# A retention head's output: copied to SBUF before it is normalised, backward scaled K on another engine, transposes back later

## The chip, the cores and the metric

The kernel runs on one core of a Trainium2 chip. A core has five engines with queues of their own: TensorE (PE, matmuls and transposes into PSUM), VectorE (DVE), ScalarE (ACT), GpSimd (POOL) and SyncE (SP, which issues the DMAs). [...] The metric is the time on the device of one execution in microseconds, the median of the runs shown.

## The reference

The kernel is one inference step of a backbone of two layers with 1024 features, on 128 prompt tokens and 512 sample tokens. Each layer normalises its input, projects it (`z = h @ w_in`), feeds three groups of mixers side by side (four retention heads, a Hyena convolution, a gated linear recurrence called RG-LRU), multiplies each by its SiLU gate and projects back. The change touches the retention heads. Each is computed in chunks of 128 tokens, forward and backward, and its output is normalised over the 128 features of the head:

```
scores = einsum('bnihd,bnjhd->bnhij', qc, kc) * dmat
inner  = einsum('bnhij,bnjhe->bnihe', scores, vc)
kv     = einsum('bnjhd,hj,bnjhe->bnhde', kc, zeta, vc)   # K scaled by zeta, per direction
cross  = einsum('bnihd,hi,bnhde->bnihe', qc, xi, R_prev) # R: running sum of kv
out    = of + ob[:, ::-1]
out    = out * lax.rsqrt(jnp.mean(out * out, axis=-1, keepdims=True) + EPS)
...
y = concat([ret_out * silu(g_r), hy_out * silu(g_h), lru_out * silu(g_l)])
```

## The kernel before

Both token groups are held together as 640 columns (five chunks of 128; with pads 644), features on the partitions. The input projection runs as a long row of matmuls: for each group of 128 output features (tile `z`) the two parts of the input (`hh`, `hl`) meet the two parts of the weights (`w_3h`, `w_3l` and so on). ScalarE rounds the weights for the high part, and GpSimd subtracts it for the low part (`split`, L830: a 128x1024 instruction for each group).

The order of TensorE's work is written out by hand: helpers `mm` (L332) and `tr` (L335) chain each matmul behind the one emitted before it and move a clock of estimated TensorE time; each mixer is a generator that yields how many microseconds of that clock to let pass before it emits its next step, and the `z` matmuls are emitted in between. Instructions of the other engines are put in order by the scheduler, by their place in the program and by a priority (`tc.high_priority`). ScalarE's work goes through one helper (`act`, L299), so that all of its rows have one line.

A retention head goes through these steps (`ret`, for layer `l` and head `h`; the tiles bear both numbers, so `rk01s` is layer 0, head 1):

- the input of a head, `ret_in`: Q and K are rotated by `rope` (VectorE L1161 and L1163, GpSimd L1162 between them);
- `rk`: K is transposed chunk by chunk into PSUM (512 columns in the tile that ends in `s`, 128 in the one that ends in `p`), and VectorE scales it into KF (forward) and KB (backward), L1199 and L1200;
- `rv`: V is transposed, and ScalarE copies it out;
- `rs`: the scores, multiplied by the decay mask on VectorE (L1218); `kv`: the chunk states, accumulated on VectorE (L1232); `ro`: the output, 3 matmuls a chunk, in PSUM;
- the normalisation: squares from PSUM on ScalarE, sums on VectorE (L1251, L1252), the power -1/2 on GpSimd (L1253), and the product of PSUM and that factor on VectorE, for 512 columns in L1254 and 128 in L1256;
- `rt`: the normalised output is transposed back and copied out by ScalarE; when both it and its gate are there, VectorE multiplies them (L1368), and the output projection reads the product at the end of the layer.

The tiles rk, rv, rs, kv, ro, rt and the gates of the RG-LRU (`lg`) take turns in four PSUM buffers; a new one waits until the readers of the oldest are done. The RG-LRU (`lru`) runs between the heads: gate matmuls `lg` (three for each group of ScalarE activations), products and two scans on VectorE (L1326 to L1349; L1342 and L1344 are the scans, L1349 adds them) and small copies of pads on GpSimd (L1337). L1208 is the scaling of Q on GpSimd. ScalarE loads a table when its function changes.

Of the kernel before, what the change touches and what calls it, by code (L numbers as in the profile page):

```python
# [12 lines left out]
AF = mybir.ActivationFunctionType  # L13
ALU = mybir.AluOpType
AX = mybir.AxisListType

P = 128
# [194 lines left out]
XQ, PW3, PA0, NA, NV, NQ, PO, PFO = 1, 0, 2, 14, 225, 1, 0, 1  # L212
PT0, PT1, PT2 = 2, 5, 8

PRI = 400
LTE, XSEQ, LA3, LH1_, LH2_, LA02, LHD, LHD0, LT0 = 2.5, 'FNAAAAAABANBAFBBBBABBB', 0.0, 3.5, 12.0, 16.0, 6.75, 76.25, 3.37
LT1, LF0, LF1, LC0, LC1, LA, LA0, LH0 = 6.25, 6.75, 3.25, 1.42, 1.31, 3.0, 11.75, 5.88
LH1, LV0, LV01, LV1, LV2, LV3, LV4, LVE, LP = 7.28, 7.5, 5.5, 3.12, 2.5, 1.71, 4.15, 9.0, 6.0
LRI, LR0, LR1, LR2, LR3, LLS, LLF, LL0 = 1.05, 1.71, 3.2, 5.7, 11.5, 1.25, 8.38, 2.83
# [5 lines left out]
def step_kernel(ctx: ExitStack, tc: tile.TileContext, xT, ada_w, w_in, w_out, vecs, fw1, fw2, fw3, lgw, sret,  # L225
                c_fwd, c_inv, c_ident, c_rope, c_ret, c_zfeat, c_win, o_y, o_ret, o_lru, dbg=None):
    nc = tc.nc
    V, S, G, T = nc.vector, nc.scalar, nc.gpsimd, nc.tensor
# [39 lines left out]
    def ar(off, n, p0=0, p1=P):  # L268
        if off >= RT_:
            return RT[0][p0:p1, off - RT_:off - RT_ + n]  # L270
        return A[p0:p1, off:off + n]
# [26 lines left out]
    def act(out, in_, f=AF.Identity, bias=0.0, scale=1.0):  # L298
        return S.activation(out, in_, f, bias=bias, scale=scale)  # L299
# [793 lines left out]
    zgs_ = [small(16) for _ in range(DEPTH)]  # L1093
# [57 lines left out]
    NO_ = SC_R + 640  # L1151
    SQ_ = ZB_ + 652
# [18 lines left out]
    read, out_, norm_ = {}, {}, {}  # L1171
# [23 lines left out]
    def ret(l, h):  # L1195
        pk, pkp = to_time(ar(K_, ZC), f"rk{l}{h}")
        for dst, i in ((KF_, h), (KB_, 4 + h)):
            with tc.high_priority(offset=PRI):
                V.tensor_scalar(ar(dst, 512), pk, ar(zgs_[l] + 2 * i, 1), None, op0=ALU.mult)  # L1199
                V.tensor_scalar(ar(dst + 512, 128), pkp, ar(zgs_[l] + 2 * i, 1), None, op0=ALU.mult)  # L1200
        if h == 0:
            yield LR1
        pv, pvp = to_time(ar(VC_, ZC), f"rv{l}{h}")
# [8 lines left out]
        for s0, blocks in ((0, (0, 1, 2, 3)), (4, (4,))):  # L1212
            nb = len(blocks)
            ps = pat(f"rs{l}{h}{s0}")
            for n in blocks:
                c = S0 + 128 * n if n < 4 else 0
# [28 lines left out]
        if h < 3:  # L1245
            ret_state(l, h + 1)
        out_[l, h] = True
        act(ar(SQ_, 512), ps, AF.Square)
        act(ar(SQ_ + 512, 128), pp[:, 0:128], AF.Square)
        v = ar(vr_, 5)  # L1250
        V.tensor_reduce(v, ar(SQ_, 640).rearrange("p (n c) -> p n c", n=5), axis=AX.X, op=ALU.add)  # L1251
        V.tensor_scalar(v, v, 1.0 / 128, EPS, op0=ALU.mult, op1=ALU.add)  # L1252
        G.tensor_tensor(v, v, ar(mh_, 5), op=ALU.pow)  # L1253
        i = V.tensor_tensor(ar(NO_, 512).rearrange("p (n c) -> p n c", n=4), ps.rearrange("p (n c) -> p n c", n=4),  # L1254
                        v[:, 0:4].unsqueeze(2).broadcast_to([P, 4, 128]), op=ALU.mult)
        norm_[l, h] = i, V.tensor_scalar(ar(NO_ + 512, 128), pp[:, 0:128], v[:, 4:5], None, op0=ALU.mult)  # L1256
        yield LR3
        pt, pp = pat(f"rt{l}{h}s"), pat(f"rt{l}{h}p")
        for n in range(5):
            tr(pt[:, 128 * n:128 * n + 128] if n < 4 else pp[:, 0:128], ar(NO_ + 128 * n, 128), ident)  # L1260
# [441 lines left out]
```

## Time and profile before

| what | value |
|---|---|
| median of 3 runs (lowest, highest) | 1303.76 us (1303.5, 1305.56) |
| the profiled execution: its own time, its span | 1307.67 us, 1305.9 us |
| mean granted TensorE clock | 0.955 of full speed |
| busy: PE, DVE, ACT, POOL | 1160.9, 893.0, 633.3, 595.5 us |
| stage of layer 0 that holds the retention heads | about 415 to 625 us of the span |
| the same stage of layer 1 | about 1025 to 1235 us |

The busy times are sums over the whole span; they don't say where an engine waits. The rows below are read by stage: the waits of one engine, the rows of an engine in order of time (its start, its duration, and in square brackets how long the engine stood idle before it and what ended the wait), and busy time with the granted clock by stretches. A row with x4 is four instructions.

### The profile page before, as it was taken

To read this page: it belongs to the slowest core of one execution; us is meant where nothing else is said; L and a number is where in the kernel's file an instruction comes from. 1 tells how busy PE (TensorE), PEld (TensorE's weight loads), DVE (VectorE), ACT (ScalarE), POOL (GpSimd) and SP (SyncE) were. 2 spreads that over 40 slices of the span, in tenths; PEclk is the share of its full clock that TensorE was granted. 3 is DMA by queue.
4 is the path that set the end of the run, shared out by engine and by line. 5 is a ranking of instruction groups with operands and counts; after the bars stand their busy time and mean duration, and the time that the engine had idled before them with its cause. 6 is when DMAs were issued, how large, how long until landed. Compare 5 with 4: busy or idle time off the path is not lost. (4 is left out here: it accounts for less than half of the span.)

```text
span 1305.9 us, 20607 instructions
## 1 busy us (share of the span) xinstructions
PE 1160.9 (89%) x7944; PEld 1099.8 (84%) x7944; DVE 893.0 (68%) x1382; ACT 633.3 (48%) x1120; POOL 595.5 (46%) x523
## 2 busy tenths in 40 slices
PE   4599988798999888898999899999999889889996
PEld 2478878797999888897787788999998889888996
DVE  5998983866776776777888775466467577666313
ACT  3566646564333765565566554332333367655220
POOL 1743335645556434524343355545355554344431
PEclk9799988999999888899999989999999899899998
DMA  9562213222121211243545464222221111213222
GB/s 336 205 204 74 77 65 143 92 91 98 55 73 48 65 35 47 79 141 115 166 145 185 130 213 136 73 80 89 66 88 42 61 49 57 65 43 120 72 62 81
DMA packets 53522, 132.80 MB, mean 102 GB/s; under 512 B 6358, under 2 KB 15590, under 8 KB 52144
## 3 DMA queue, kind: packets, MB, share of 16 engines
q1 hardware_dynamic: 53076, 131.38, 30.7%
q8 instruction: 62, 1.02, 0.3%
q14 instruction: 36, 0.29, 0.1%
q10 hardware_dynamic: 348, 0.11, 0.0%
HBM read 112.77 MB, written 18.70 MB: 101 GB/s over the span
## 5 line engine op out<-in xcount | busy, mean ns | idle before, releaser
L299 ACT ACTIVATE arena<-arena 128x644 f32<-128x644 f32 (+6 forms) x168 | 116.6, 722 | 80.1 <-DVE arena L1400 28.3
L299 ACT ACTIVATE r<-arena 128x512 fp32r<-128x512 f32 (+1 forms) x72 | 43.6, 605 | 90.1 <-DVE arena L519 34.2
L299 ACT ACTIVATE rt<-arena 128x512 fp32r<-128x512 f32 (+2 forms) x44 | 29.7, 674 | 76.0 <-POOL arena L983 50.5
L332 PE MATMUL u<-r,cfwd 128*128 128x256 f32 x432 | 61.6, 291 | 2.1 <-DVE r L544 1.9
L544 POOL TENSOR_TENSOR r<-arena,r 128x512 fp32r<-128x512 f32 (+1 forms) x24 | 29.3, 1220 | 70.0 <-ACT r L299 53.5
L332 PEld LDWEIGHTS u<-r,cfwd 128*128 128x128 f32 x432 | 57.4, 199 | 3.1 <-DVE r L544 2.5
L1400 DVE SCALAR_TENSOR_TENSOR arena<-o,arena 128x128 f32<-128x128 f32 (+3 forms) x34 | 16.7, 524 | 56.0 <-PE o L332 56.0
L332 PE MATMUL lg<-r 128*128 128x322 f32 x192 | 39.0, 360 | 10.4 <-DVE rt L1199 8.4
L978 DVE TENSOR_TENSOR arena<-u,arena 128x512 f32<-128x512 f32 x40 | 27.4, 686 | 30.1 <-PE u L332 30.1
L983 POOL TENSOR_TENSOR arena<-arena 128x256 f32<-128x256 f32 x40 | 37.0, 926 | 20.1 <-DVE arena L979 13.5
L332 PEld LDWEIGHTS lg<-r 128*128 128x128 f32 x192 | 35.5, 230 | 12.3 <-issue 8.9
L332 PE MATMUL spr<-r,cfwd 128*128 128x256 f32 x192 | 35.0, 293 | 11.1 <-ACT rt L299 6.4
L332 PE MATMUL spi<-r,cfwd 128*128 128x256 f32 x168 | 36.2, 304 | 7.0 <-ACT r L299 4.2
L986 POOL TENSOR_TENSOR rt<-arena,rt 128x512 fp32r<-128x512 f32 x24 | 31.2, 1302 | 24.0 <-ACT rt L299 24.0
L332 PEld LDWEIGHTS spr<-r,cfwd 128*128 128x128 f32 x192 | 27.8, 189 | 16.9 <-ACT rt L299 8.4
L299 ACT ACT_TABLE_LOAD x30 | 38.5, 1283 | 3.9 <-DMA arena<-in_vecs 3.4
L299 ACT ACTIVATE r<-rt 128x512 fp32r<-128x512 f32 (+3 forms) x50 | 28.2, 565 | 22.7 <-PE spi L332 11.7
L544 POOL TENSOR_TENSOR r<-rt,r 128x256 fp32r<-128x256 f32 (+1 forms) x16 | 19.7, 1229 | 42.6 <-ACT r L299 36.0
L544 POOL TENSOR_TENSOR dm<-rt,r 128x256 fp32r<-128x256 f32 (+1 forms) x16 | 22.5, 1408 | 33.7 <-ACT r L299 33.7
L299 ACT ACTIVATE arena<-lg,arena 128x322 f32<-128x322 f32 x64 | 30.9, 529 | 14.4 <-PE lg L332 13.9
L1319 POOL MEMSET arena<- 128x2 f32 x32 | 2.1, 100 | 77.9 <-ACT arena L299 77.9
L332 PEld LDWEIGHTS spi<-r,cfwd 128*128 128x128 f32 x168 | 27.9, 200 | 11.4 <-ACT r L299 4.9
(1266 smaller groups left out, 4177.6 us busy)
## 6 DMA issues: line engine op xcount, KB each, us to landing
w<-in_w_in SPq DMA_DIRECT2D x80, 512.0 KB
aw<-in_ada_w SPq DMA_DIRECT2D x96, 256.0 KB
wo<-in_w_out SPq DMA_DIRECT2D x32, 384.0 KB
spec<-arena SPq DMA_DIRECT2D x16, 640.0 KB
arena<-spec SPq DMA_DIRECT2D x8, 1280.0 KB
arena<-in_xT SPq DMA_DIRECT2D x16, 320.0 KB
rt<-in_c_win SPq DMA_DIRECT2D x4, 640.0 KB
arena<-xspill SPq DMA_DIRECT2D x8, 320.0 KB
```

The source lines that it names most:

```text
L299: return S.activation(out, in_, f, bias=bias, scale=scale)
L332: return queue(T.matmul(out, lhs, x, start=start, stop=stop), w * n / 2400 * (4 if x.dtype == F32 else 1))
L544: eng.tensor_tensor(lo, src, f(h), op=ALU.subtract)
L978: V.tensor_tensor(y, pv, hre[:, c].unsqueeze(1).broadcast_to([P, 2, 256]), op=ALU.mult)
L983: G.tensor_tensor(y[:, 1], y[:, 1], m2[:, 0], op=ALU.add)
L986: (G if PY >> c & 1 else V).tensor_tensor(lo, yo, f(h), op=ALU.subtract)
L1319: G.memset(ar(tt[d] + c, 2), 1.0)
L1400: V.scalar_tensor_tensor(x, zc(ps, pc, pc + n), ar(mod_[l] + 32 + 2 * mt + s, 1), x, op0=ALU.mult, op1=ALU.add)
```

## The change

A head's output is copied from PSUM to SBUF by ScalarE at once (two copies with a priority), squared from there by one instruction, and the product with the factor is one VectorE instruction in place, SBUF by SBUF, over all 640 columns. KB is written by ScalarE and KF by VectorE as before. After the product, heads 0 to 2 let 14.0 us pass instead of 11.5 before they emit their transposes back; head 3 still 11.5.

```diff
--- before.py
+++ after.py
@@ -212,7 +212,7 @@
 XQ, PW3, PA0, NA, NV, NQ, PO, PFO = 1, 0, 2, 14, 225, 1, 0, 1
 PT0, PT1, PT2 = 2, 5, 8
 
-PRI = 400
+PRI, LR4 = 400, 14.0
 LTE, XSEQ, LA3, LH1_, LH2_, LA02, LHD, LHD0, LT0 = 2.5, 'FNAAAAAABANBAFBBBBABBB', 0.0, 3.5, 12.0, 16.0, 6.75, 76.25, 3.37
 LT1, LF0, LF1, LC0, LC1, LA, LA0, LH0 = 6.25, 6.75, 3.25, 1.42, 1.31, 3.0, 11.75, 5.88
 LH1, LV0, LV01, LV1, LV2, LV3, LV4, LVE, LP = 7.28, 7.5, 5.5, 3.12, 2.5, 1.71, 4.15, 9.0, 6.0
@@ -1196,8 +1196,13 @@
         pk, pkp = to_time(ar(K_, ZC), f"rk{l}{h}")
         for dst, i in ((KF_, h), (KB_, 4 + h)):
             with tc.high_priority(offset=PRI):
-                V.tensor_scalar(ar(dst, 512), pk, ar(zgs_[l] + 2 * i, 1), None, op0=ALU.mult)
-                V.tensor_scalar(ar(dst + 512, 128), pkp, ar(zgs_[l] + 2 * i, 1), None, op0=ALU.mult)
+                g = ar(zgs_[l] + 2 * i, 1)
+                if i < 4:
+                    V.tensor_scalar(ar(dst, 512), pk, g, None, op0=ALU.mult)
+                    V.tensor_scalar(ar(dst + 512, 128), pkp, g, None, op0=ALU.mult)
+                else:
+                    act(ar(dst, 512), pk, scale=g)
+                    act(ar(dst + 512, 128), pkp, scale=g)
         if h == 0:
             yield LR1
         pv, pvp = to_time(ar(VC_, ZC), f"rv{l}{h}")
@@ -1245,16 +1250,18 @@
         if h < 3:
             ret_state(l, h + 1)
         out_[l, h] = True
-        act(ar(SQ_, 512), ps, AF.Square)
-        act(ar(SQ_ + 512, 128), pp[:, 0:128], AF.Square)
+        with tc.high_priority(offset=PRI):
+            act(ar(NO_, 512), ps)
+            act(ar(NO_ + 512, 128), pp[:, 0:128])
+        act(ar(SQ_, 640), ar(NO_, 640), AF.Square)
         v = ar(vr_, 5)
         V.tensor_reduce(v, ar(SQ_, 640).rearrange("p (n c) -> p n c", n=5), axis=AX.X, op=ALU.add)
         V.tensor_scalar(v, v, 1.0 / 128, EPS, op0=ALU.mult, op1=ALU.add)
         G.tensor_tensor(v, v, ar(mh_, 5), op=ALU.pow)
-        i = V.tensor_tensor(ar(NO_, 512).rearrange("p (n c) -> p n c", n=4), ps.rearrange("p (n c) -> p n c", n=4),
-                        v[:, 0:4].unsqueeze(2).broadcast_to([P, 4, 128]), op=ALU.mult)
-        norm_[l, h] = i, V.tensor_scalar(ar(NO_ + 512, 128), pp[:, 0:128], v[:, 4:5], None, op0=ALU.mult)
-        yield LR3
+        norm_[l, h] = [V.tensor_tensor(ar(NO_, 640).rearrange("p (n c) -> p n c", n=5),
+                                       ar(NO_, 640).rearrange("p (n c) -> p n c", n=5),
+                                       v.unsqueeze(2).broadcast_to([P, 5, 128]), op=ALU.mult)]
+        yield LR3 if h == 3 else LR4
         pt, pp = pat(f"rt{l}{h}s"), pat(f"rt{l}{h}p")
         for n in range(5):
             tr(pt[:, 128 * n:128 * n + 128] if n < 4 else pp[:, 0:128], ar(NO_ + 128 * n, 128), ident)
```

The lines after L1199 have other numbers in the new kernel (L1254 becomes L1261, L1251 L1258, L1252 L1259, L1344 L1351, L1348 L1355, L1349 L1356, L1368 L1375). Three places show how the order moves.

VectorE, before the product of head 2 and the last rope add of head 3's K. `ro02s` is head 2's output in PSUM, `lr` a recurrence, `rt` the K to be rotated, `arena` other SBUF. Before:

```order
L1251 TENSOR_REDUCE arena<-arena 128x5
L1344 SCALAR_TENSOR_TENSOR arena<-arena 128x644
L1252 TENSOR_SCALAR arena<-arena 128x5
L1348 COPY arena<-arena 128x1
L1349 TENSOR_TENSOR lr_3370<-lr_3370,arena 128x644
L1368 TENSOR_TENSOR lr_3370<-lr_3370,arena 128x644
L1161 TENSOR_TENSOR rt_3875<-z_7_4823,arena 128x512
L1254 TENSOR_TENSOR arena<-ro02s,arena 128x512
L1163 TENSOR_TENSOR rt_3875<-rt_3875,arena 128x512
```

After:

```order
L1351 SCALAR_TENSOR_TENSOR arena<-arena 128x644
L1354 COPY arena<-lr_3370 128x1
L1311 TENSOR_TENSOR r_97<-lr_3453,r_97 128x644
L1258 TENSOR_REDUCE arena<-arena 128x5
L1355 COPY arena<-arena 128x1
L1356 TENSOR_TENSOR lr_3370<-lr_3370,arena 128x644
L1259 TENSOR_SCALAR arena<-arena 128x5
L1375 TENSOR_TENSOR lr_3370<-lr_3370,arena 128x644
L1161 TENSOR_TENSOR rt_3875<-z_7_4823,arena 128x512
L1261 TENSOR_TENSOR arena<-arena 128x640
L1163 TENSOR_TENSOR rt_3875<-rt_3875,arena 128x512
```

The old order has the sum of squares (L1251) ahead of the backward scan, and the scale-and-add of the mean (L1252) behind it; the recurrence's copy and add (L1348, L1349) come next. In the new order the scan, the copy and the add (L1355, L1356) are ahead of L1259, and the product L1261 reads and writes SBUF alone.

ScalarE, head 0 to 1, with what each instruction waits for (`rv01s` and `rk01s` are the transposed V and K of head 1, `lg` a gate of the recurrence, `z` a projection tile). Before:

```order
L299 ACTIVATE arena<-z_9_4196 128x644 [waits PE_49]
L299 ACTIVATE rt_3875<-rv01s 128x512 [waits PE_49]
L299 ACTIVATE rt_3875<-rv01p 128x128 [waits PE_49]
L299 ACT_TABLE_LOAD [waits DVE_49]
L299 ACTIVATE arena<-lg_4326,arena 128x322 [waits PE_49]
```

After:

```order
L299 ACTIVATE arena<-z_9_4196 128x644 [waits PE_49]
L299 ACTIVATE rt_3875<-rv01s 128x512 [waits PE_49]
L299 ACTIVATE rt_3875<-rk01s,arena 128x512 [waits DVE_49]
L299 ACTIVATE rt_3875<-rk01p,arena 128x128 [waits DVE_49]
L299 ACTIVATE rt_3875<-rv01p 128x128 [waits PE_49]
L299 ACT_TABLE_LOAD [waits PE_49]
L299 ACTIVATE arena<-lg_4326,arena 128x322 [waits Pool_49]
```

The two instructions for KB (out of `rk01s` and `rk01p`) stand between the copies of V, and wait for VectorE's event. The table load waited for VectorE and now waits for TensorE.

TensorE, head 2 to 3, from the transposes of head 3's V on (`rt02` transposes head 2's output back; `z_12` is a projection group). Before:

```order
L335 MATMUL rv03s<-arena 128x128 x4
L335 MATMUL rv03p<-arena 128x128
L335 MATMUL rt02s<-arena 128x128 x4
L335 MATMUL rt02p<-arena 128x128
L332 MATMUL z_12_4989<-hh_423,w_12h 128x322 x2
L332 MATMUL z_12_4989<-hl_424,w_12h 128x322 x2
L332 MATMUL lg_5036<-r_97 128x322 x3
L332 MATMUL lg_5041<-r_97 128x322 x3
L332 MATMUL lg_5046<-r_97 128x322 x3
L332 MATMUL lg_5051<-r_97 128x322 x3
L332 MATMUL rs_5062<-rt_3875 128x128 x4
L332 MATMUL rs_5068<-rt_3875 128x128
```

After:

```order
L335 MATMUL rv03s<-arena 128x128 x4
L335 MATMUL rv03p<-arena 128x128
L332 MATMUL z_12_4989<-hh_423,w_12h 128x322 x2
L332 MATMUL z_12_4989<-hl_424,w_12h 128x322 x2
L332 MATMUL z_12_4989<-hh_426,w_12h 128x322 x2
L332 MATMUL z_12_4989<-hl_427,w_12h 128x322 x2
L332 MATMUL lg_5028<-r_97 128x322 x3
L332 MATMUL lg_5033<-r_97 128x322 x3
L332 MATMUL lg_5038<-r_97 128x322 x3
L332 MATMUL lg_5043<-r_97 128x322 x3
L335 MATMUL rt02s<-arena 128x128 x4
L335 MATMUL rt02p<-arena 128x128
```

The transposes back go from in front of the gates to behind them, and two more projection pairs go ahead of the gates (in the old order they stood behind the scores). At head 1 to 2 the transposes rt01 stood ahead of head 2's `rk02` and now stand behind the gates likewise.

## Rows read from the trace of the kernel before

**Rows 1.** Table of stretches: us, busy of each engine (count), TensorE clock, DMA share, GB/s
```profile
460.00:475.00 15.00, 9.95 (x51) 9.07 (x50) 8.04 (x14) 6.50 (x10) 5.89 (x9) 0.77 0.12 36
475.00:503.00 28.00, 28.00 (x202) 27.94 (x201) 23.37 (x31) 18.66 (x31) 15.75 (x16) 1.00 0.15 48
```
**Rows 2.** Waits of TensorE, 415 to 625 us: total us, times, longest
```profile
PE rk03s L335 <- DVE rt L1163: 4.5, 1, 4.5
...
PE rv01s L335 <- DVE arena L1254: 3.7, 1, 3.7
PE rt01p L335 <- DVE arena L1256: 3.5, 1, 3.5
```
**Rows 3.** The same table, 1035 to 1200 us (layer 1)
```profile
PE rk13s L335 <- DVE rt L1163: 4.5, 1, 4.5
```
**Rows 4.** TensorE, head 0 to 1: start us, us, engine, line, operation [idle before]
```profile
468.80 3.59 PE L332 MATMUL lg<-r 128*128 128x322 f32 x12 [0.47 <-ACT rt L299]
...
475.26 1.94 PE L332 MATMUL lg<-r 128*128 128x322 f32 x12
```
**Rows 5.** VectorE, head 0 to 1
```profile
466.19 0.69 DVE L1254 TENSOR_TENSOR arena<-ro00s,arena 128x512 f32<-128x512 f32 x1 [1.30 <-POOL arena L1253]
466.80 0.34 DVE L1256 TENSOR_SCALAR arena<-ro00p,arena 128x128 f32<-128x128 f32 x1
467.06 1.40 DVE L1199 TENSOR_SCALAR rt<-rk01s,arena 128x512 f32<-128x512 f32 x2
...
474.64 0.89 DVE L1218 TENSOR_TENSOR arena<-rs,dm 128x512 f32<-128x512 f32 x2 [5.66 <-PE rs L332]
```
**Rows 6.** GpSimd, head 0 to 1
```profile
464.97 1.19 POOL L1253 TENSOR_TENSOR arena<-arena 128x5 f32<-128x5 f32 x1
466.13 2.37 POOL L830 TENSOR_TENSOR w_6l<-w,w_6h 128x1024 fp32r<-128x1024 f32 x1
```
**Rows 7.** ScalarE, head 0 to 1
```profile
454.34 0.60 ACT L299 ACTIVATE arena<-ro00s 128x512 f32<-128x512 f32 x1 [0.78 <-PE ro00s L332]
...
458.19 1.06 ACT L299 ACTIVATE w_6h<-w 128x1024 fp32r<-128x1024 f32 x1 [3.08 <-issue]
...
468.15 0.60 ACT L299 ACTIVATE rt<-rv01s 128x512 f32<-128x512 f32 x1 [6.91 <-PE rv01s L335]
...
468.93 1.28 ACT L299 ACT_TABLE_LOAD   x1
```
**Rows 8.** VectorE, head 1 to 2
```profile
498.11 0.82 DVE L1349 TENSOR_TENSOR lr<-lr,arena 128x644 f32<-128x644 f32 x1
...
500.31 0.68 DVE L1254 TENSOR_TENSOR arena<-ro01s,arena 128x512 f32<-128x512 f32 x1
503.58 2.82 DVE L1163 TENSOR_TENSOR rt<-rt,arena 128x512 f32<-128x512 f32 x1 [2.59 <-POOL arena L1162]
```
**Rows 9.** GpSimd, head 1 to 2
```profile
499.93 2.40 POOL L830 TENSOR_TENSOR w_3l<-w,w_3h 128x1024 fp32r<-128x1024 f32 x1
502.29 1.26 POOL L1162 TENSOR_TENSOR arena<-arena 128x512 f32<-128x512 f32 x1
503.52 2.33 POOL L830 TENSOR_TENSOR w_7l<-w,w_7h 128x1024 fp32r<-128x1024 f32 x1
```
**Rows 10.** TensorE, heads 1 to 2 and 2 to 3
```profile
506.88 0.60 PE L335 MATMUL rk02s<-arena,rt 128*128 128x128 f32 x4
...
508.71 3.59 PE L332 MATMUL lg<-r 128*128 128x322 f32 x12 [0.56 <-ACT rt L299]
...
518.65 1.95 PE L332 MATMUL kv<-rt 128*128 128x128 f32 x16
...
547.18 1.12 PE L335 MATMUL rk03s<-arena,rt 128*128 128x128 f32 x4 [4.54 <-DVE rt L1163]
...
558.74 1.95 PE L332 MATMUL kv<-rt 128*128 128x128 f32 x16
```
**Rows 11.** VectorE, the backward scan ahead of head 2 to 3
```profile
537.25 1.50 DVE L1344 TENSOR_TENSOR_SCAN arena<-arena 128x644 f32<-128x644 f32 x1 [0.50 <-POOL arena L1337]
```

## The prediction

> **What bounds the kernel now.** I read the table of waits first, over the projection stage of layer 0 (415 to 625 us) and of layer 1 (1035 to 1200 us), then TensorE's rows around each wait, then VectorE's, GpSimd's and ScalarE's rows at the same times, last the table of stretches. TensorE is the engine that ends last in this stage: in the 28.00 us from 475 to 503 it is busy for all 28.00 at a granted clock of 1.00, the upper of its two levels (2.4 GHz) [rows 1]. It stops only where one retention head hands over to the next. The waits are 3.7 us before rv01s (head 0 to 1), 3.5 us before rt01p (1 to 2), 4.5 us before rk03s (2 to 3) [rows 2], and layer 1 repeats all three within 0.1 us, of which one row stands here [rows 3]. Each stop costs twice: the mean granted clock is 0.77 in 460 to 475 [rows 1], and twelve gate matmuls (tile lg) take 3.59 us right after the stop against 1.94 us later, at the upper level [rows 4]. So the question is when TensorE is released at each handover, and how far behind it then is. Six handovers count (three a layer). The first head (rk00) has nobody in front of it, and the last one hands over to nobody.
>
> **What happens at a handover now.** Rows of 0 to 1: VectorE ends the mean of squares (L1252), GpSimd's pow runs until 464.97 + 1.19 = 466.16, VectorE multiplies the PSUM tile by it (L1254, 466.19, 0.69 us), then L1256, and only then are the buffers of ro00 free for rv01. KF and KB follow (L1199, two in 1.40 us) [rows 5, 6]. The gates start at 468.80 and end at 468.80 + 3.59 = 472.39 [rows 4].
>
> **The change part by part.**
> *The copies of ro to SBUF.* ScalarE's copy of this shape from PSUM is the old Square, 0.60 us; the short one I take as half of it, 0.3. They stand where the two Squares stood [rows 7]. The new Square over 640 columns in SBUF is one more, 0.8 us by the 0.82 of a similar size on VectorE [rows 8]. ScalarE's gaps there cover it (the gate activations come 14 us later). Cost 0; gain: rv01s no longer waits for L1254, so the 3.7 us stop goes from that place. What is late next is the gate matmuls, which take the buffers that KF and KB read.
>
> *The norm moves from PSUM to SBUF.* One VectorE instruction of 128x640 with two SBUF inputs takes the place of 0.69 + 0.34 us [rows 5]. Undisturbed I take 0.82, from the 128x644 add L1349 [rows 8]. But pow releases it at 466.16, and GpSimd's next instruction, the weight split w_6l, runs from 466.13 to 468.50 [rows 6]. The rows show what that does. The VectorE add L1163, whose two inputs are both in SBUF, starts at 503.58 beside the split w_7l (503.52 to 505.85) and takes 2.82 us, until 0.55 us after the split has ended; L1254 with one PSUM input at 500.31, beside w_3l (499.93 to 502.33), takes its 0.68 [rows 8, 9]. So the new multiply should end at about 468.50 + 0.75 = 469.25 where L1254 ended at 466.88. Bounds: 0.82 us if nothing blocks it, 2.37 + 0.82 = 3.2 if the whole split does; I take 3.1, from the L1163 row, which is the same situation.
> The Trainium skill (SBUF — State Buffer, "Who interferes with whom") says that VectorE and GpSimd share one pair of SBUF ports under an exclusive lock, and that a VectorE instruction with at most one SBUF input doesn't need it. By that rule the old multiply was free of GpSimd and the new one is not; the two rows agree with it. By the rule the time is the forecast's below; a reading without it gives the multiply 0.82 and the time of the rival in which nothing changes.
>
> *KB on ScalarE.* Four VectorE instructions become two; ScalarE's two take 0.60 and 0.3. The VectorE time saved (0.70, and 0.34 by L1256 for the 128 columns) falls into idle time: after KF and KB it waits 5.66 us for the scores [rows 5]. KB reads the same PSUM tile as KF and in ScalarE's queue waits for VectorE. Behind it stand the short copies of KB and rv, the table load and the gates' activations. KB ends one ScalarE instruction after the first KF.
>
> *Handover 0 to 1.* 469.25 + 0.70 (KF) + 0.60 (KB) = 470.55, so the second gate group can start at 470.6; the first needs only rv01s and runs before. Nine matmuls remain at 3.59/12 = 0.30: 2.7 us, until 473.3 against 472.39: **+0.9 us**. Without the block it would be 466.19 + 0.82 + 0.70 + 0.60 + 2.7 = 471.0: -1.4.
>
> *Handover 1 to 2.* In the new order VectorE runs the RG-LRU add (L1349 before, 0.82 us, and a one-column copy) ahead of the mean of squares; everything after, pow, split, L1162, the rope add, is later by about 0.85. The blocked norm stands ahead of L1163 in VectorE's queue and beside L1162 on GpSimd, which now follows the split at once (502.29) [rows 9]: another 0.7. Against that, rt01p no longer stands between the rope add and rk02 (add done at 506.40, rk02s at 506.88), and one z group fills the 0.56 us before the gates [rows 10]: 0.85 of the 12.25 us from rope add to kv (518.65). Sum **+0.7**.
>
> *Handover 2 to 3.* The same +0.85 and +0.7. The backward scan (L1344) no longer waits its 0.50 us for GpSimd's copies, which now stand ahead of the q scaling [rows 11]: -0.5. From rk03s (547.18) to kv (558.74) are 11.6 us [rows 10]. The table load, 1.28 us, ran in TensorE's stop; now it waits for the first gate group, so all gate activations follow it: +1.28. One z group, four matmuls of a gate's shape at 1.94/12 = 0.16 [rows 4], moves from behind kv to ahead of it: -0.6. Sum 0.85 + 0.7 - 0.5 + 0.6 = **+1.65**.
>
> *Later transposes.* This step issues five transposes, two GpSimd memsets and two ScalarE copies, no DMA; their reader is the output projection's split, long after. Cost 0 for rt00; for rt01 and rt02 the orders above have it in them. If that cover were gone, five transposes of 128 columns, at most 1.12 us by the row of rk03s [rows 10], would come onto the path per head.
>
> One layer: 0.9 + 0.7 + 1.65 = 3.25; two layers 6.5. After head 3 TensorE has no stop of this size until the output projection, so the shift carries through. The profiled execution took 1307.67 us (span 1305.9), so it would take 1314.2; the median of the runs is 3.9 lower, so 1303.76 + 6.5 = **1310.3 us**.
>
> **Rivals.**
> *Faster: the chain through VectorE is shorter.* If the shared stretch with GpSimd doesn't decide and VectorE's queue does, each handover loses the two KB (1.04) and L1256 (0.34) and gains 0.82 - 0.69 = 0.13: about 1.2 us; less some for KB's hop to ScalarE, 1.05 us at six handovers is 6.3: 1297.5 us. For it: the rows of the 3.7 us stop, in which ro00's release is the last event. Against: GpSimd's split is already running when pow's result is there, in both handovers whose rows stand here [rows 6, 8, 9].
> *No change: the norm isn't blocked.* 0 to 1 gives -1.4, 1 to 2 gives 0, 2 to 3 gives +0.95: -0.45 a layer, 1302.9 us, inside what can't be told from none. For it: the split could start a little after the norm. Against: 466.13 is before 466.16.
> *Slower still: ScalarE's queue becomes the bound.* KB stands ahead of the table load, rv's short copy and the gate activations on ScalarE. If each handover pays for KB's two instructions a second time through that queue (0.6 of 0.9), 6 x 0.6 = 3.6: 1314 us. It decides once the first gate group's activation waits for KB longer than for TensorE. Against: ScalarE stands 3.08 us idle before a split there, and its wait at rv01s is much of the stage [rows 7].
>
> **How the numbers follow.** Forecast 0.46 (its own range 1306.5 to 1313), faster 0.22, no change 0.22, slower still 0.10. What a measurement of this kernel can tell from no change is 0.2%, 2.6 us. Forecast and slower still together are 0.56 on the slower side. The range has to hold 8 of 10: from 1299.0, which leaves out about half of the faster case, to 1315.5, above the slower still. Its ends also hold the bounds of the norm (0.82 to 3.2 us).
>
> **What would show it.** In the new trace the 128x640 multiply (L1261) takes 2.5 to 3.2 us where a split runs beside it, and 0.8 where none does; TensorE's wait at rv01s and rt01p is gone; new waits stand before lg, released by ScalarE's KB, of 3 us or more at 0 to 1, and before rk02s and rk03s, longer by about 1.5 us than the old rk03s wait. I am wrong if L1261 takes 0.82 after pow, or if lg runs at the upper clock level in the handovers, for then the stops have gone and the time is under 1303.

## The result, and the profile after

The changed kernel takes 1317.09 us (median of 4 runs, 1314.89 to 1321.39) against 1304.66 us (1303.5 to 1305.91, 4 runs) for the kernel before on the same occasions: a ratio of 1.0097, with a 95% interval from 1.0074 to 1.0121. It is 12.4 us slower. The forecast was slower by 6.5 us, 1310.3, and the range ended at 1315.5: the sign is right, the size is about half of what came, and the time lies 1.6 us above the range.

The profiled execution took 1314.89 us (span 1313.1), 7.2 more than that of before. Its part ahead of the retention heads happened to be 3.3 us shorter (the first rk00s starts at 419.4 instead of 422.7), so the two spans can't be compared as a whole, and the stage is compared head by head. The table gives the time from the first matmul of a head's output (tile ro) to that of the next, in us; one column is one handover.

| kernel | layer 0: 0 to 1 | 1 to 2 | 2 to 3 | layer 1: 0 to 1 | 1 to 2 | 2 to 3 |
|---|---|---|---|---|---|---|
| before | 35.1 | 40.4 | 40.1 | 33.6 | 40.3 | 39.8 |
| after | 37.1 | 42.1 | 42.3 | 37.1 | 42.1 | 42.2 |
| difference | +2.0 | +1.7 | +2.2 | +3.5 | +1.8 | +2.4 |
| forecast | +0.9 | +0.7 | +1.65 | +0.9 | +0.7 | +1.65 |

The six differences add up to 13.6 us. What TensorE waits for, first in layer 0 (415 to 630 us), then in layer 1 (1030 to 1245), in us in total, times and longest; it answers to [rows 2, 3]:

```profile
PE lg L332 <- ACT rt L299: 10.4, 3, 5.6
PE rk03s L335 <- DVE rt L1163: 6.0, 1, 6.0
PE rk02s L335 <- DVE rt L1163: 5.9, 1, 5.9
```

```profile
PE lg L332 <- ACT rt L299: 10.7, 3, 5.6
PE rk13s L335 <- DVE rt L1163: 6.0, 1, 6.0
```

The waits before rv01s and rt01p are gone. In their places stand one of 5.6 us before the gates (lg, released by ScalarE's KB) and one of 5.9 us before rk02s, and the one before rk03s has grown from 4.5 to 6.0. (Of the lg row's 10.4 us, 4.2 belong to head 0 and were there before.)

GpSimd, VectorE and ScalarE of the new kernel at head 0 to 1, each in order of time, answering to [rows 5 to 7]:

```profile
461.61 1.19 POOL L1260 TENSOR_TENSOR arena<-arena 128x5 f32<-128x5 f32 x1 [0.82 <-PE lg L332]
462.76 2.35 POOL L830 TENSOR_TENSOR w_6l<-w,w_6h 128x1024 fp32r<-128x1024 f32 x1
```

```profile
462.83 2.96 DVE L1261 TENSOR_TENSOR arena<-arena 128x640 f32<-128x640 f32 x1 [1.30 <-POOL arena L1260]
465.71 0.74 DVE L1201 TENSOR_SCALAR rt<-rk01s,arena 128x512 f32<-128x512 f32 x1
```

```profile
466.48 0.69 ACT L299 ACTIVATE rt<-rk01s,arena 128x512 f32<-128x512 f32 x1 [5.66 <-DVE rt L1201]
```

The power ends at 462.80, the weight split starts at 462.76, and the product L1261 takes 2.96 us, until 0.68 us after the split has ended. It takes this long in all eight heads (2.96 to 3.02). KF starts when it is done, KB one VectorE instruction later. TensorE at the same place, answering to [rows 4]:

```profile
460.88 0.71 PE L332 MATMUL lg<-r 128*128 128x322 f32 x3 [0.58 <-ACT rt L299]
467.22 2.78 PE L332 MATMUL lg<-r 128*128 128x322 f32 x9 [5.63 <-ACT rt L299]
...
470.88 2.33 PE L332 MATMUL rs<-rt 128*128 128x128 f32 x10
```

The first gate group runs early, as foreseen, and the other nine matmuls start 5.63 us later. What was not foreseen follows them. The table of stretches of before and of after, around head 0 to 1 of layer 0 and of layer 1 (us, busy time of PE, PEld, DVE, ACT, POOL, then the granted clock, the DMA share and GB/s):

```profile
467.00:473.50 6.50, 6.00 (x23) 5.62 (x24) 1.98 (x5) 4.71 (x8) 1.50 (x1) 0.50 0.28 83
...
1078.00:1081.50 3.50, 3.03 (x13) 2.63 (x13) 1.79 (x4) 2.58 (x4) 1.29 (x1) 0.51 0.32 92
```

```profile
463.00:473.50 10.50, 6.28 (x26) 6.28 (x27) 4.38 (x5) 5.80 (x10) 2.38 (x5) 0.51 0.14 50
...
1077.50:1087.50 10.00, 5.67 (x24) 5.67 (x24) 3.88 (x4) 5.80 (x10) 2.49 (x5) 0.50 0.16 52
```

Before, the clock was at its lower level for 6.5 us in layer 0 and 3.5 us in layer 1 after a stop of 3.7 us. Now it is at the lower level for 10.5 and 10 us, and already during the stop.

### The profile page after: what moved, and what is told of

It reads as the page before. It is cut to its first block, busy times and chain, and to the rows that moved or that the text cites. A ratio compares the mean times of both kernels' runs of the same rounds, so it can differ in the third digit from the quotient of the medians.

```text
span 1313.1 us, 20598 instructions
## 1 busy us (share of the span) xinstructions
PE 1156.3 (88%) x7944; PEld 1094.5 (83%) x7944; DVE 902.2 (69%) x1358; ACT 644.0 (49%) x1144; POOL 603.2 (46%) x523
## 5 line engine op out<-in xcount | busy, mean ns | idle before, releaser
L299 ACT ACTIVATE arena<-arena 128x644 f32<-128x644 f32 (+7 forms) x176 | 122.3, 723 | 81.0 <-DVE arena L1407 28.4
L332 PEld LDWEIGHTS lg<-r 128*128 128x128 f32 x192 | 32.8, 214 | 23.5 <-ACT rt L299 22.6
L1335 DVE SCALAR_TENSOR_TENSOR arena<-arena,lr 128x644 f32<-128x644 f32 x16 | 13.2, 828 | 49.0 <-ACT arena L299 49.0
L983 POOL TENSOR_TENSOR arena<-arena 128x256 f32<-128x256 f32 x40 | 37.1, 927 | 19.5 <-DVE arena L979 12.8
L299 ACT ACTIVATE r<-rt 128x512 fp32r<-128x512 f32 (+3 forms) x50 | 28.2, 564 | 21.4 <-PE spi L332 11.3
```

The lines of the kernel that those rows point to most:

```text
L332: return queue(T.matmul(out, lhs, x, start=start, stop=stop), w * n / 2400 * (4 if x.dtype == F32 else 1))
L983: G.tensor_tensor(y[:, 1], y[:, 1], m2[:, 0], op=ALU.add)
L1335: V.scalar_tensor_tensor(ar(ti[d], ZC), ar(ti[d], ZC), 1.0, u, op0=ALU.add, op1=ALU.mult)
```

## The experiments

The change has three parts: the output copied to SBUF and normalised there, KB on ScalarE, the transposes back later. (PSUM is the memory that TensorE writes; in these traces VectorE and ScalarE read it out into SBUF, and no row of GpSimd reads it.) Three runs undo one part each; two more put one part alone on the kernel before. The others test what delays the handovers. Ratios are to the kernel before run at the same time, with 95% intervals.

**KB on VectorE again, the rest of the change kept.**

```diff
-                if i < 4:
-                    V.tensor_scalar(...)  # KF
-                else:
-                    act(ar(dst, 512), pk, scale=g)
-                    act(ar(dst + 512, 128), pkp, scale=g)
+                V.tensor_scalar(ar(dst, 512), pk, g, None, op0=ALU.mult)
+                V.tensor_scalar(ar(dst + 512, 128), pkp, g, None, op0=ALU.mult)
```

> The changed kernel with both scaled copies of K on VectorE again (the other two parts of the change stay). Theory A (the product of the norm, now SBUF by SBUF, waits for GpSimd's weight split and stands ahead of KF in VectorE's queue): no gain, 1314 to 1320 us; the product still takes about 2.97 us and the second gate group starts 5 to 6 us late at head 0 to 1. Theory B (KB's hop to ScalarE and what queues behind it there is the loss): back to 1302 to 1308 us.

Measured: 1313.76 us, 1.0068 (1.0048 to 1.0089). Most of the loss stays, so KB's way over ScalarE is not its main cause; the time came out 0.2 us under the interval that theory A gave, and the gates at head 0 to 1 still wait, 5.1 us. The whole change has 1.0097 (1.0074 to 1.0121): the intervals overlap, so whether a smaller part, up to 0.3%, is KB's stays open.

**The transposes back early again, the rest kept.**

```diff
-        yield LR3 if h == 3 else LR4
+        yield LR3
```

> The changed kernel with the transposes back emitted after 11.5 us as before for every head (the other two parts stay). Theory A (blocked norm): no gain, 1314 to 1321 us; rt01 stands ahead of rk02 again but both wait for the same rope add and norm. Theory C (the moved transposes and what they let go ahead cost the time): back to 1302 to 1308 us.

Measured: 1318.6 us, 1.0098 (1.0077 to 1.0119). The loss is the same without the later transposes, so they aren't the cause.

**The product out of PSUM again, KB on ScalarE and the later transposes kept.**

```diff
-        with tc.high_priority(offset=PRI):
-            act(ar(NO_, 512), ps)
-            act(ar(NO_ + 512, 128), pp[:, 0:128])
-        act(ar(SQ_, 640), ar(NO_, 640), AF.Square)
+        act(ar(SQ_, 512), ps, AF.Square)
+        act(ar(SQ_ + 512, 128), pp[:, 0:128], AF.Square)
...
-        norm_[l, h] = [V.tensor_tensor(ar(NO_, 640)..., ar(NO_, 640)..., ...)]
+        i = V.tensor_tensor(ar(NO_, 512)..., ps..., ...)
+        norm_[l, h] = i, V.tensor_scalar(ar(NO_ + 512, 128), pp[:, 0:128], ...)
```

> KB on ScalarE and the later transposes stay, but the head's output is squared and multiplied out of PSUM again as before the change. Theory A (blocked norm): the product takes 0.69 us again and the time is 1301 to 1308 us. Theories B and C (KB on ScalarE, later transposes): stays at 1314 to 1320 us.

Measured: 1302.24 us, 0.9975 (0.9963 to 0.9988): the loss is gone, and a little more. VectorE's product in this kernel, at head 0 to 1:

```profile
462.63 0.69 DVE L1259 TENSOR_TENSOR arena<-ro00s,arena 128x512 f32<-128x512 f32 x1 [1.30 <-POOL arena L1258]
...
463.49 0.74 DVE L1201 TENSOR_SCALAR rt<-rk01s,arena 128x512 f32<-128x512 f32 x1
```

It takes 0.69 us as before, and KF follows 2.0 us sooner after the product's start than in the changed kernel (0.86 against 2.88 us).

At heads 1 to 2 and 2 to 3 the waits before rk02s and rk03s are 3.8 and 3.7 us here, against 5.9 and 6.0 in the changed kernel. VectorE ahead of the power at 1 to 2, and then GpSimd's rope step, in the changed kernel:

```profile
495.04 1.65 DVE L1311 TENSOR_TENSOR r<-lr,r 128x644 fp32r<-128x644 f32 x1
496.61 0.81 DVE L1258 TENSOR_REDUCE arena<-arena 128x5 f32<-128x640 f32 x1
...
498.13 0.15 DVE L1259 TENSOR_SCALAR arena<-arena 128x5 f32<-128x5 f32 x1
```

```profile
502.39 1.84 POOL L1162 TENSOR_TENSOR arena<-arena 128x512 f32<-128x512 f32 x1
```

VectorE in the kernel with the product out of PSUM:

```profile
492.83 0.79 DVE L1256 TENSOR_REDUCE arena<-arena 128x5 f32<-128x640 f32 x1
...
494.40 0.16 DVE L1257 TENSOR_SCALAR arena<-arena 128x5 f32<-128x5 f32 x1
494.47 0.82 DVE L1309 TENSOR_TENSOR r<-lr,r 128x644 fp32r<-128x644 f32 x1
```

So about 1.5 of the 2.1 us at 1 to 2 come from VectorE's order: in the changed kernel a product of the recurrence (L1311, 1.65 us) stands ahead of the mean of squares, and here behind it (L1309). The other 0.6 us is GpSimd's rope step, 1.84 us beside the SBUF product and 1.26 here. No run changes that order alone.

**Either of the other parts alone, on the kernel before.** KB on ScalarE (the diff's first hunk in `ret` and nothing else), and the later transposes:

```diff
-        yield LR3
+        yield LR3 if h == 3 else LR4
```

> The kernel before with KB on ScalarE and nothing else. The run with this and the later transposes was 0.25% faster than before. If KB brought it: 1300 to 1304 us. If the later transposes did: 1303 to 1308 us, as before (KB ends as early on either engine).

> The kernel before with the transposes back emitted after 14.0 us for heads 0 to 2 and nothing else. If the later transposes brought the 0.25%: 1300 to 1304 us, with the wait before rt01p gone and one of about 3.8 us before rk02 in its place. If KB did: 1303 to 1308 us.

Measured: KB on ScalarE 1305.69 us, 1.0017 (1.0005 to 1.003); the later transposes 1300.99 us, 0.9977 (0.9966 to 0.9987). The gain comes with the later transposes. TensorE's waits in layer 0 with them alone:

```profile
PE rk02s L335 <- DVE rt L1163: 3.8, 1, 3.8
PE rk03s L335 <- DVE rt L1163: 3.7, 1, 3.7
```

The 3.5 us before rt01p have become 3.8 before rk02s, and the wait before rk03s is 0.8 us shorter than before [rows 2]. VectorE's order moves here too: the recurrence's product (L1304), ahead of the mean of squares in the kernel before, stands behind it, so the gain isn't TensorE's order alone. Set against these, the part that goes through SBUF costs 0.9% beside the later transposes alone (from 0.9977 to 1.0068), 0.8% beside KB alone (1.0017 to 1.0098) and 1.2% beside both (0.9975 to 1.0097). That part by itself was not run.

**The product behind the next head's KF.** One order is added to the changed kernel:

```diff
-                    V.tensor_scalar(ar(dst + 512, 128), pkp, g, None, op0=ALU.mult)
+                    kf = V.tensor_scalar(ar(dst + 512, 128), pkp, g, None, op0=ALU.mult)
+                    for j in norm_.get((l, h - 1), ()):
+                        behind(j, kf)
```

> The changed kernel with one order added: the product of the norm goes behind the next head's KF in VectorE's queue. Theory A (blocked norm ahead of KF and of the rope add): at head 0 to 1 KF runs as soon as rk01 is there, so of the 5.6 us wait before the second gate group at most 1 us stays and the clock's low stretch behind it goes; at the other two handovers the wait loses only 0.6 us, since GpSimd's split and the rope's GpSimd step stay in their places. About 9 to 10 us a layer in all: 1294 to 1302 us. Theories B and C: no gain, 1314 to 1320 us.

Measured: 1305.77 us, 1.0008 (0.9988 to 1.0029). The mechanism is as theory A has it and the size is not: 11.3 us come back, and the time is 3.8 us above the upper end of what was expected. TensorE's gates at head 0 to 1, and VectorE's products at head 0 to 1 and 1 to 2:

```profile
464.08 2.71 PE L332 MATMUL lg<-r 128*128 128x322 f32 x9 [1.37 <-ACT rt L299]
```

```profile
462.55 0.75 DVE L1201 TENSOR_SCALAR rt<-rk01s,arena 128x512 f32<-128x512 f32 x1
...
463.94 2.99 DVE L1263 TENSOR_TENSOR arena<-arena 128x640 f32<-128x640 f32 x1 [0.38 <-POOL arena L1262]
...
504.27 0.81 DVE L1263 TENSOR_TENSOR arena<-arena 128x640 f32<-128x640 f32 x1
```

KF (462.55) no longer waits for the power; the 5.6 us stop is 1.37. The same instruction, two SBUF inputs, 640 columns, takes 2.99 us beside a GpSimd split and 0.81 where GpSimd stands idle. By the table's measure head 0 to 1 is 31.6 and 31.7 us long, but the other two are 41.5 to 41.8, nearly as in the changed kernel: there the power and the split still stand ahead of the rope's GpSimd step. The product's place is worth 0.4 to 0.7 us at each of these two.

**The split behind the product.** The product no longer meets the split that follows the power: a one-column copy on GpSimd that reads the product stands ahead of the split that followed the power.

```diff
+        tiny = G.tensor_copy(ar(hold_, 1), ar(NO_, 1))
+        nm = f"w{l}_{(6, 3, 12, 15)[h]}"
+        HOLD[nm] = tiny
+        if nm in SPL:
+            behind(SPL[nm], tiny)
...   # and in split(): a split that is emitted later goes behind its HOLD
```

> The changed kernel with GpSimd's next weight split (for w_6, w_3, w_12, w_15) put behind the product of the norm, by a one-column GpSimd copy that reads the product. The scheduler then also lets the rope's GpSimd step at heads 1 to 2 and 2 to 3 run ahead of that split. Theory A (the split that is already running when the power is done holds up the product and, behind it, KF or the rope add): the product takes about 0.82 us at every head where no GpSimd instruction runs beside it, the second gate group of head 0 to 1 starts about 2.1 us earlier, the waits before rk02 and rk03 fall from 5.9 to about 2 us; 1293 to 1303 us. Theory E (the product in SBUF is slow by itself, or the copies on ScalarE are what costs): 1313 to 1320 us.

Measured: 1289.98 us, 0.9886 (0.9866 to 0.9907), better than expected. VectorE at head 0 to 1 and its product at 1 to 2, then TensorE at 0 to 1 and at 1 to 2:

```profile
464.30 0.82 DVE L1267 TENSOR_TENSOR arena<-arena 128x640 f32<-128x640 f32 x1 [1.30 <-POOL arena L1266]
...
498.19 1.90 DVE L1267 TENSOR_TENSOR arena<-arena 128x640 f32<-128x640 f32 x1 [0.46 <-POOL arena L1266]
```

```profile
466.56 2.78 PE L332 MATMUL lg<-r 128*128 128x322 f32 x9 [3.49 <-ACT rt L299]
```

```profile
500.75 0.66 PE L335 MATMUL rk02s<-arena,rt 128*128 128x128 f32 x4 [1.49 <-DVE rt L1169]
```

The product takes 0.82 us at head 0 to 1, the stop there is 3.49 instead of 5.63 (2.1 less, as foreseen), and the one before rk02s is 1.49 instead of 5.93. At 1 to 2 the product runs beside GpSimd's rope step and takes 1.90 us. Not all of the gain is the hold-up by the split: GpSimd's rope step now runs ahead of the split, and 1 to 2 and 2 to 3 are shorter (36.5 to 36.6 us in both layers). What the hold-up alone is worth reads from head 0 to 1, where the instructions stand in the changed kernel's order but for the split: 37.1 to 33.8 us in layer 0 and to 34.8 in layer 1. That contains the slow clock behind the longer stop (the scores take 1.28 us instead of 2.33). The copies on ScalarE stay in this run, so theory E falls.

**The product in five instructions with one SBUF tensor each.**

```diff
-        norm_[l, h] = [V.tensor_tensor(ar(NO_, 640)..., ar(NO_, 640)..., ...)]
+        norm_[l, h] = [V.tensor_scalar(ar(NO_ + 128 * n, 128), ar(NO_ + 128 * n, 128), v[:, n:n + 1], None, op0=ALU.mult)
+                       for n in range(5)]
```

> The changed kernel with the product done by five VectorE instructions of 128 columns, each with one SBUF tensor and a factor per partition, in place of one with two SBUF tensors. Theory A1 (only two tensor inputs in SBUF are held up by GpSimd): the five take about 1.3 us together beside the split, the second gate group of head 0 to 1 starts 1.6 us earlier than in the changed kernel; 1309 to 1315 us. Theory A2 (any VectorE instruction from SBUF to SBUF is held up by the split): the five take 3 us or more, 1315 to 1322 us.

Measured: 1317.53 us, 1.0095 (1.0077 to 1.0112): theory A2. The forty instructions' shortest, median and longest in ns, and the first five in the order of time:

```profile
L1261 DVE TENSOR_SCALAR arena<-arena x40: 272/274/2422, 465.7 to 1200.6; 128x128 f32<-128x128 f32 x40
```

```profile
465.75 3.14 DVE L1261 TENSOR_SCALAR arena<-arena 128x128 f32<-128x128 f32 x5 [1.30 <-POOL arena L1260]
```

One of the five takes up to 2422 ns, the others 0.27 us: the first waits for the split and the rest follow. My reading of the rows, that two SBUF tensors are what makes an instruction wait, was too narrow.

**The product on ScalarE.**

```diff
-        norm_[l, h] = [V.tensor_tensor(ar(NO_, 640)..., ar(NO_, 640)..., ...)]
+        norm_[l, h] = []
+        for n in range(5):
+            act(ar(NO_ + 128 * n, 128), ar(NO_ + 128 * n, 128), scale=v[:, n:n + 1])
```

> The changed kernel with the product done by ScalarE, in five instructions of 128 columns with a factor per partition. Theory A (the product on VectorE is held up and holds up KF): the wait before the second gate group of head 0 to 1 falls from 5.6 to about 1.4 us as in the run with the product behind KF, the five take about 1.3 us beside the split since ScalarE isn't held up by GpSimd, the waits before rk02 and rk03 fall by 0.6 us only; 1301 to 1309 us. Theory E (copies and extra work on ScalarE cost the time): 1317 to 1325 us.

Measured: 1316.32 us, 1.0094 (1.0075 to 1.0113). The time is not theory A's, and the reason is not quite theory E's. ScalarE at head 0 to 1 and its product at 1 to 2, GpSimd's split at 1 to 2, and TensorE at 0 to 1:

```profile
465.40 1.57 ACT L299 ACTIVATE arena<-arena 128x128 f32<-128x128 f32 x5 [10.54 <-POOL arena L1260]
466.88 1.04 ACT L299 ACTIVATE w_6h<-w 128x1024 fp32r<-128x1024 f32 x1
...
501.91 1.57 ACT L299 ACTIVATE arena<-arena 128x128 f32<-128x128 f32 x5 [8.58 <-POOL arena L1260]
```

```profile
501.85 2.34 POOL L830 TENSOR_TENSOR w_3l<-w,w_3h 128x1024 fp32r<-128x1024 f32 x1
```

```profile
468.56 1.12 PE L335 MATMUL rv01s<-arena 128*128 128x128 f32 x4 [6.24 <-ACT arena L299]
```

At 1 to 2 the five run beside the split w_3l and take 1.57 us, as long as at 0 to 1, where no split runs beside them (w_6l starts at 468.05, behind the rounding). VectorE's KF is early (464.01), as theory A has it. But in ScalarE's queue the five stand ahead of the rounding of w_6 and of a projection tile's copy, and the queue waits 10.54 us for the power; rv01s, which transposes what that copy writes, waits 6.24. At 1 to 2 and 2 to 3 the waits before rk02s and rk03s shrink to 1.7 us and less, and projection groups wait 4.0 us instead. The waits went to another queue.

**The whole chain of the norm behind the rope.** The sum of squares goes behind the next head's last rope add, and the product behind KF:

```diff
+        rop_[l, h] = i
+        if (l, h - 1) in red_:
+            behind(red_[l, h - 1], i)
...   # i is the rope's last add, red_ the sum of squares; the product goes behind KF as above
```

> The changed kernel with two orders added: the sum of squares goes behind the next head's last rope add on VectorE, and the product of the norm behind the next head's KF. The power on GpSimd then comes after the rope's GpSimd step, and the split before that step is not held up by it. Theory A (what delays the handovers is the norm's chain standing in front of the rope add and of KF, and GpSimd's lock): the waits before rk02 and rk03 fall from 5.9 us to under 2 us, the one before the second gate group to about 1.4 us; 1276 to 1292 us. Theory D (the wait before rk02 and rk03 is set by the RG-LRU's work on VectorE, not by the norm): as the run with the product alone behind KF, 1303 to 1309 us.

Measured: 1290.86 us, 0.9902 (0.9884 to 0.992), in the range of theory A. The waits before rk02s and rk03s are gone; projection groups now wait 2.1 and 2.3 us at the two places for the rope's first product (L1161). It starts at 499.40 at heads 1 to 2, and VectorE and GpSimd show what is ahead of it:

```profile
494.69 2.96 DVE L1365 TENSOR_TENSOR lr<-lr,arena 128x644 f32<-128x644 f32 x1
497.69 1.79 DVE L1384 TENSOR_TENSOR lr<-lr,gt 128x644 f32<-128x644 f32 x1
```

```profile
493.98 2.98 POOL L830 TENSOR_TENSOR w_3l<-w,w_3h 128x1024 fp32r<-128x1024 f32 x1
496.93 1.86 POOL L1162 TENSOR_TENSOR arena<-arena 128x512 f32<-128x512 f32 x1
```

The recurrence's add (L1365) and its gate product (L1384) take 2.96 and 1.79 us beside the split w_3l and the rope's GpSimd step; in the kernel before the same two take 0.82 [rows 8] and 0.83.

**The same with four low parts of weights a layer on VectorE.**

```diff
+        if mt in (3, 7, 12, 13):
+            eng = V
```

> The kernel with the sum of squares behind the rope add and the product behind KF (1290.9 us), with the low parts of the weights w_3, w_7, w_12 and w_13 computed by VectorE (about 1.1 us each) instead of GpSimd (2.4 us each, during which VectorE's SBUF work stands). Theory A: the RG-LRU's add and gate product no longer take 2.96 and 1.79 us beside the split, the wait before the projection group at heads 1 to 2 and 2 to 3 (2.3 us each) falls under 1 us; 1282 to 1290 us. Rival: VectorE's own load takes the place of the hold-up; 1290 to 1297 us.

Measured: 1282.2 us, 0.9827 (0.9803 to 0.9851), the best kernel of all, 22 us below the one before. The line numbers are two higher here: L1163 is the rope's first product, L1367 the recurrence's add. The subtraction takes VectorE 1.22 us:

```profile
492.16 1.84 DVE L1367 TENSOR_TENSOR lr<-lr,arena 128x644 f32<-128x644 f32 x1
...
494.79 1.22 DVE L830 TENSOR_TENSOR w_3l<-w,w_3h 128x1024 fp32r<-128x1024 f32 x1
```

```profile
PE z L332 <- DVE rt L1163: 2.8, 2, 1.5
```

The two waits before projection groups fall from 2.3 to 1.5 us at most, not under 1 (one of the two instructions named still takes 1.84 us, beside the rope's GpSimd step). Here VectorE does more work and the kernel is faster. Two things changed at once: VectorE no longer stands beside these splits, and GpSimd's queue is shorter. Which of them brought how much is not shown.

**Matmuls in the stop.** The changed kernel with 40 more matmuls of 190 columns after the first gate group of head 0 to 1; their results aren't used.

```diff
+                    if ct == 1 and d == kind == n == 0:
+                        for _ in range(40):
+                            mm(pg[:, HC:512], gh[:, c0:c0 + 128], uh[:, 0:512 - HC], start=True, stop=True, w=0.0)
```

> The changed kernel with 40 more TensorE matmuls of 190 columns (their results are not used) between the first and the second gate group of head 0 to 1 in both layers, in the 5.6 us in which TensorE waits for KB there. They take about 4 us and delay nothing that waits for VectorE. Theory F (the part that the forecast lacks is the lower clock level that follows a longer stop, 10.2 us long here against 6.8 and 3.4 us before): the granted clock stays 1.00 through head 0 to 1, the nine gate matmuls take 1.5 us instead of 2.8, and the time falls by 3 to 4 us a layer; 1309 to 1312 us. Theory G (the lack is elsewhere, the clock follows the stop without setting the time): 1315 to 1320 us.

Measured: 1316.19 us, 1.009 (1.0075 to 1.0105): in theory G's range, too small a gain to tell from none. The trace tells more. TensorE at head 0 to 1, and the table of stretches there:

```profile
461.93 5.16 PE L332 MATMUL lg<-r 128*128 128x322 f32 x43 [0.58 <-ACT rt L299]
468.33 1.61 PE L332 MATMUL lg<-r 128*128 128x322 f32 x9 [1.24 <-ACT rt L299]
```

```profile
463.00:474.00 11.00, 9.70 (x75) 9.27 (x75) 5.55 (x6) 6.38 (x12) 3.48 (x6) 1.00 0.15 48
```

The clock stays at 1.00, the nine matmuls take 1.61 us instead of 2.78, and head 0 to 1 is 34.8 us long in both layers, 2.3 less than in the changed kernel. So the lower level costs 2.3 us a layer there. Of that 1.1 us a layer are lost again at 2 to 3 (43.3 us instead of 42.2). The first two lines are TensorE's gates and the clock there in this run, the last one the gates in the changed kernel:

```profile
551.89 2.59 PE L332 MATMUL lg<-r 128*128 128x322 f32 x12
547.50:553.00 5.50, 5.45 (x23) 5.45 (x24) 1.01 (x2) 1.62 (x5) 0.00 (x0) 0.50 0.23 72
...
552.57 1.92 PE L332 MATMUL lg<-r 128*128 128x322 f32 x12
```

After a stop of the same length before rk03s (5.94 and 5.95 us) the clock is at its lower level for 5.5 us more here, and for 2.6 us more (548.88 to 551.50) in the changed kernel, and the twelve gate matmuls take 2.59 us instead of 1.92. ScalarE's instructions come in the same order in both. So the lower level takes back there what it no longer costs at 0 to 1, in part; why it lasts longer is open. What is left, 2.4 us in all, is inside what the runs of this kernel spread over.

## Why the prediction was right or wrong

Right were the direction and the chain behind it. The split that is running when the power is done holds up the new product (forecast 3.1 us, measured 2.96 to 3.02), the wait moves from rv01s to the gates, the waits before rk02s and rk03s are 1.4 to 1.5 us longer than the old one before rk03s (forecast about 1.5), and the second gate group starts 8.2 us after rk01s (467.22 after 458.99), which in the times of before is 470.8; forecast 470.6. For head 0 to 1 the cause is shown: with the split behind the product it is 3.3 and 2.3 us shorter than in the changed kernel, and with the product out of PSUM again 34.8 and 34.4 us long instead of 37.1. The Trainium skill's rule (SBUF — State Buffer, "Who interferes with whom") agrees with the sign. The page limits what it says of an instruction with at most one SBUF input to those "outside the 2-port perf modes". The prediction left that condition out; the run with five instructions shows that it matters, though not for the product as it was changed.

Wrong was the size. The sum has 3.25 us a layer; measured are 5.9 in layer 0 and 7.7 in layer 1. Three terms are too small, and a fourth is wrong the other way.

- *Handover 0 to 1, +0.9.* Measured +2.0 and +3.5; this is the largest miss. The forecast went up to the last of the nine gate matmuls (473.3 against 472.39) and let what follows run as before. It took the low clock for these nine alone; but the stop is now one of 5.6 us instead of one of 3.7, and the low level lasts 10.5 and 10 us in place of 6.5 and 3.5. And layer 1 was taken to be like layer 0, since its waits are alike to 0.1 us; its low stretch is half as long, so it had more to lose. The run with matmuls in the stop prices the whole low stretch at 2.3 us a layer. The scores, which come after the gates, take 2.33 us; in layer 0 of the kernel before they took 1.56:

```profile
473.26 1.56 PE L332 MATMUL rs<-rt 128*128 128x128 f32 x10
```

- *Handover 1 to 2, +0.7.* Measured +1.7 and +1.8. rk02s came 1.6 to 1.8 us later, near the 1.55 of the two delays, but in part by luck: counted from ro01s, the rope add of layer 0 ended about 2.2 us later, and 0.4 of that came back because rt01p no longer stands between it and rk02s, which the forecast had counted in its gain of 0.85. The rest of that gain did not come: from rk02s to ro02s it is 20.0 to 20.3 us in both kernels and layers. Four of the five transposes rt01 ran ahead of the stop in the kernel before (at 502.59); now all five stand in this stretch, between the gates and the scores, and take 1.2 us with their wait:

```profile
512.86 0.66 PE L335 MATMUL rt01s<-arena 128*128 128x128 f32 x4 [0.33 <-ACT arena L299]
```

- *Handover 2 to 3, +1.65.* Measured +2.2 and +2.4. From rk03s to kv it came as forecast (12.1 us instead of 11.6). The 0.5 us wait of the backward scan went, but the scan now runs beside GpSimd's Q scaling and takes 2.37 us, against 0.50 + 1.50 before [rows 11]: 0.4 us lost where 0.5 was to be gained. VectorE's row:

```profile
534.48 2.37 DVE L1351 TENSOR_TENSOR_SCAN arena<-arena 128x644 f32<-128x644 f32 x1
```

- *Later transposes, 0.* Alone they make the kernel before 0.23% faster, 1300.99 against 1303.59 us in the same rounds. This doesn't explain the missing loss: it means that the SBUF part costs more, 1.2% beside the other two parts, than the difference of the two kernels shows.

That the loss belongs to the SBUF part is shown by the combinations. That it is the hold-up of the product is shown for 0 to 1 alone, which has 5.5 of the 13.6 us. At 1 to 2 and 2 to 3 the product's place is worth 0.4 to 0.7 us each; the rest is VectorE's order ahead of the power and the scan's longer time, read from the rows and tested by no run of its own. How much of the loss there is low clock and how much stop is not separated either: no run kept TensorE busy there.

Of the rivals, "no change" fell with the product's 2.96 us. "Slower still" came nearest in size and had the wrong place: with KB on VectorE again most of the loss stays. "Faster" assumed that the length of VectorE's queue decides. A gain of 1% does come once the norm stands behind KF and the rope add; whether that order would gain as much without the change was not run.

## What to carry to other kernels

In this kernel, moving a VectorE operand from PSUM to SBUF freed the PSUM buffer, but exposed the instruction to what GpSimd ran at that moment (2.96 us instead of 0.82). Look up which GpSimd instruction is released by the same event, and what stands behind the exposed instruction in VectorE's queue. When a value is no longer needed early, say so in the order: here the copy that releases the buffer came with a gain only when the work behind it was moved out of the way too. And a forecast that joins two stops into one has to price the clock after the stop from rows at either level, in each layer for itself, and up to the place where the clock has risen again. A change of one instruction can also let the scheduler reorder its neighbours: compare the whole order ahead of the wait, not only the instruction that was changed.

## What the runs showed of the hardware that I had not expected

VectorE's TENSOR_SCALAR from SBUF to SBUF in fp32, with one tensor input, waits for a GpSimd instruction just as TENSOR_TENSOR does: 2422 ns at most against 272 alone. The Trainium skill allows for it in the same section (SBUF — State Buffer, "Who interferes with whom"): `tensor_scalar` is among the operations that can enter a two-port mode and then contend with GpSimd. I had read only its neighbour, the sentence on one SBUF input. With a PSUM input it was not held up: in the kernel before, KF and KB run beside the split w_6l and take 1.40 us for two [rows 5, 6].

The subtraction of a 128x1024 weight takes GpSimd about 2.35 us and VectorE 1.22, and on GpSimd it cost VectorE up to 2.2 us of standing beside it (the product's 3.02 us instead of 0.82).

The low clock after a stop differs between places with equal stops: 6.5 and 3.5 us after 3.7 us in the two layers of one execution of the kernel before, and, before rk03s, 2.6 us in the changed kernel and 5.5 us in the run with matmuls in the stop, after a stop of 5.9 us in both.
